# Moving a weight fold ahead of two gate blocks, splitting output weights on GpSimd, and keeping rotary tables in rotating small buffers

## The chip, the cores and the metric

The kernel runs on one core of a Trainium2 chip. The metric is the device time of one execution in microseconds, lower is better; the time before is the median of three runs. The engines are TensorE (PE, with its weight loads PEld), VectorE (DVE), ScalarE (ACT), GpSimd (POOL) and SyncE (SP), which issues most DMAs. A "q" behind an engine's name (SPq) is its instruction queue.

## The reference

One step of a two-layer hybrid backbone on 1024 latent and 256 context tokens of width 1024, ten tiles of 128 tokens. Layer 0 is attention with a gate, layer 1 Fourier mixing with a gate. Cut to layer 0, where the change lies:

```python
hl = modulate(rms_norm(xl, norm_g[0]), shl, scl)       # the same for the context tokens
qa, ka, va, ga, qb, kb, vb, gb = split_even(hl @ even_w_in[0])
qa, ka = apply_rope(rms_norm(qa, gq)), apply_rope(rms_norm(ka, gk))
qb, kb = apply_rope(qb), apply_rope(kb)                # rotary positions, latent tokens only
oa = dense_block_attention(qa, [ka, ka_ctx], [va, va_ctx])                 # mixer A, global
ob = window_attention_with_ctx(qb, kb, vb, kb_ctx, vb_ctx, sink)           # mixer B, +-128 tokens
xl = xl + gate * (concat([oa * silu(ga), ob * silu(gb)]) @ even_w_out[0])
...
u, gate = split(h @ odd_w_in)                          # layer 1
x = x + gate * ((real(fft2(u)) * silu(gate)) @ odd_w_out)
```

## The kernel before, in words

All matrix products are in single precision split in two parts: `split` makes a high part (a rounded copy) and a low part (source minus high part) of each operand, and `mm3` runs three matmuls for a product. The strings given to `split` name the engines: "a" is ACT, "d" DVE, "p" POOL, and a longer string is a cycle.

Layer 0 runs as a stream of attention units. A unit is (tile t, group g, head pair pr): groups 0 and 1 are mixer A's key and value heads, 2 and 3 mixer B's. `soft` makes the scores on PE, their running maxima on DVE and the exponentials on ACT; `weigh` transposes the probabilities on PE (`pt`), copies them out on ACT with the low part on DVE, multiplies with the values (`av`), and leaves the result in a small buffer `e` (the copy L1060 on ACT and the sum L1062 on DVE) until a DMA to `od` (L1068) has taken it. After a tile's last unit `totals` makes the reciprocal row sums, which also pass through an `e` buffer (L1030) on their way to `scd`.

Everything else of layer 0 is filler. `fl_`, a `Filler`, holds a queue of pieces with a cost each. After every unit, `pump` adds that unit's credit (4.4 for most units of mixer A, 2.9 for mixer B's) and issues pieces from the head of the queue as long as the credit covers their cost and their `ready` condition holds; a head that is not ready holds up all behind it. The order of the queue is:

- the projections in the order of `ORDER`: query blocks `qa`, `qb`, key and value block `kb`, and the gate blocks `g0` to `g3`, each of 256 columns. `loader` loads the next block's weights ahead of the work of the block before it, and `releaser` gives a block's buffers back;
- the last two blocks, `g2` and `g3`, are taken together by token group (two groups of 512 latent tokens, then the 256 context tokens); beside the second and third group `wout_next` loads and splits the output weights `w_out`, eight row blocks of two halves each, into the buffers that the normalised input leaves;
- the fold named in `FLATE`, `f3`: `fold_load` loads 256 rows of layer 1's first weight, and four times `fold_piece` multiplies a part of it with a DFT table (PE, `wa`, 8 matmuls), copies it out on ACT and writes it to `wd`. The other three folds are made at the start of the kernel;
- the output projections `proj_load` and `proj_step` (PE, `oz`), two tiles a pair. A `proj_load` fetches a tile's `od`, gate `gd`, row sums `scd` and residual `xp`, multiplies them (L1221, L1222) and splits the product. During attention these loads are issued from POOL and the multiplies run there; only the first two pairs may begin before the attention ends.

The code gives the order of each engine's work by priority; the final static order on each engine is that of a list scheduler, which may put a later piece ahead of one that isn't ready. Within an engine, instructions run in that order.

SBUF is cut by hand into zones of equal buffers: `u`, `w`, `q`, `pt`, `p`, `h` (nine of 512 columns, for raw weights and temporaries) and `e` (four of 256 columns). `take` gives the buffer that has been free the longest, and `drop` gives one back. The rotary tables, 8 tiles of 96 columns, are a tile of their own, loaded once at L590 and read by `rope_pair`.

Of the kernel before, what the change touches and what calls it, by code (L numbers as in the profile page):

```python
# [9 lines left out]
F32 = mybir.dt.float32  # L10
# [7 lines left out]
P = 128  # L18
# [1 line left out]
NT = 10  # L20
EPS = 1e-6
GROUPS = ((0, 4, 0), (4, 4, 0), (8, 2, 1))
ZONES = {"u": (26, 1032), "w": (8, 1032), "q": (2, 1024), "pt": (3, 1024), "p": (4, 1280), "h": (9, 512), "e": (4, 256)}
BIG = ("w", "q", "pt", "p", "u")
UV = ("u",)
FILL_A, FILL_B, LAG_A, LAG_B = 4.4, 2.9, 1, 2
E_PH, E_OH, E_OL, E_WO = "a", "a", "d", "a"
# [30 lines left out]
FC, XF = 1.3, False  # L58
# [2 lines left out]
PAIRS = ((0, 4), (2, 6), (3, 7), (1, 5), (8, 9))  # L61
FILL_C, NLATE = 2.9, 8
E_FQ, E_GD = "d", "d"
ORDER = "qa0 qa1 kb0 qb0 qb1 g0 g1 g2 g3"
FLATE = "f3"
AT_B = "s"
AT_F = (0, 1, 2)
AT_N, AT_Z = (0, 0, 3, 0, 3, 2, 2, 2, 2, 2, 3, 3, 3), ("p", "pt", "q")
# [71 lines left out]
def hybrid_step(ctx: ExitStack, tc: tile.TileContext, I, O):  # L140
    nc = tc.nc
    pe, act, dve, pool, sp = nc.tensor, nc.scalar, nc.vector, nc.gpsimd, nc.sync

    cp = ctx.enter_context(tc.tile_pool(name="const", bufs=1))
# [11 lines left out]
    def take(tag, shape, dt=F32):  # L156
        tags = (tag,) if isinstance(tag, str) else tag
        z = min((t for t in tags if spare[t]), key=lambda t: spare[t][0])
        i = spare[z].popleft()[1]
        size = 2 if dt == BF16 else 4  # L160
        for s in shape[1:]:
            size *= s
        assert size <= 4 * ZONES[z][1]
        made[0] += 1
        return Buf(z, i, up.tile(list(shape), dt, tag=f"{z}{i}", name=f"{z}{made[0]}", bufs=1))

    def drop(*bufs):
        for b in bufs:
            stamp[0] += 1
            spare[b.zone].append((stamp[0], b.idx))  # L170
# [50 lines left out]
    SU = cp.tile([P, NT, 16, 2], F32, name="SU")  # L221
    NM = cp.tile([P, NT, 8], F32, name="NM")
    pool.memset(SU, 0.0)
    rope = cp.tile([P, 8, 96], F32, name="rope")

    csw = take("e", (P, 8, 32))
    pool.memset(csw.a, 0.0)
# [53 lines left out]
    def split(dst_h, dst_l, src, hc="a", lc="p"):  # L281
        copy("hi" + hc, hc, dst_h, src)
        pick("lo" + lc, lc).tensor_sub(dst_l, src, dst_h)  # L283


    def load_w(src, width=256, tags="w", gap=None, lc=E_WL, each=None, later=None):
        out = []
        for kp in range(2):
            hi = take(tags, (P, 4, width), F32R)
            lo = take(tags, (P, 4, width), F32R)  # L290
            for j in range(2):
                r0 = (kp * 4 + j * 2) * P
                if width <= 256:
                    raw = take("h", (P, 2, width))
                else:
                    raw = take(("p", "pt", "q", "w"), (P, 2, width))
                if gap is None:
                    sp.dma_start(raw.a, src[r0 : r0 + 2 * P, :].rearrange("(j p) f -> p j f", p=P))
                else:
                    gap(raw, r0)  # L300
                if each is not None:
                    each(raw, kp * 4 + 2 * j)

                def fin(raw=raw, hi=hi[:, 2 * j : 2 * j + 2, :], lo=lo[:, 2 * j : 2 * j + 2, :]):
                    split(hi, lo, raw.a, XE["wh"], lc)
                    drop(raw)

                if later is None:
                    fin()
                else:  # L310
                    later.append(fin)
            out.append((hi, lo))
        return out

    def drop_w(w):
        for h, l in w:
            drop(h, l)
# [7 lines left out]
    def w0cols(c0):  # L325
        return I["w_in0"][:, c0 : c0 + 256]
# [209 lines left out]
    def fold_load(g, parts=1):  # L536
        if "f" not in fold:
            fold["f"] = take("h", (P, 2, 256))
            sp.dma_start(fold["f"].a, I["fch"])
        wu = [take("w", (P, 1024)) for j in range(2)]  # L540
        for h in range(parts):
            cols = slice(h * (1024 // parts), (h + 1) * (1024 // parts))
            for j in range(2):
                sp.dma_start(wu[j][:, cols], I["wuT"][(2 * g + j) * P : (2 * g + j + 1) * P, cols])
        return wu
# [38 lines left out]
    def small_loads(i):  # L584
        if i == 0:
            sp.dma_start(gT, I["gT"])
            sp.dma_start(bT, I["bT"])
            dve.tensor_scalar(bT1, bT[:, :, 8:16], 1.0, None, op0=ALU.add)
        elif i == 1:
            sp.dma_start(rope, I["rope"])  # L590
            sp.dma_start(gk, I["gk"].partition_broadcast(P))
            sp.dma_start(gq, I["gq"].partition_broadcast(P))
        else:
            sp.dma_start(sink, I["sink"].partition_broadcast(P))
            dve.tensor_scalar(nsink, sink, -1.0, None, op0=ALU.mult)
            mraw = take("h", (P, 384))
            sp.dma_start(mraw.a, I["mask"])
            dve.tensor_copy(maskf, mraw.a)
            drop(mraw)
# [98 lines left out]
        drop(ck)  # L698

    def rope_pair(y, n, t, t1, t2):  # L700
        cb = rope[:, t : t + 2, 0:32].unsqueeze(2).to_broadcast([P, 2, 2 * n, 32])
        pick("rope", XE["rope"]).tensor_mul(  # L702
            t1.rearrange("p t h (b c) -> p t (h b) c", b=2), y.rearrange("p t h (b c) -> p t (h b) c", b=2), cb
        )
        for b in range(2):
            o, i = 32 * b, 32 - 32 * b
            sb = rope[:, t : t + 2, 32 + o : 64 + o].unsqueeze(2).to_broadcast([P, 2, n, 32])
            pick("rope", XE["rope"]).tensor_mul(t2[:, :, :, o : o + 32], y[:, :, :, i : i + 32], sb)
        pick("radd", XE["radd"]).tensor_add(t1, t1, t2)

# [133 lines left out]
    fl_ = Filler()  # L844
    fl_.depth = 9
    ws = {}
# [250 lines left out]
                after(u0)  # L1097
            fl_.pump(budget(un))

    def out_weights(src, ks, tags, lc="pd"):  # L1100
        out = []
        for k in ks:
            hi, lo = take(tags, (P, D), F32R), take(tags, (P, D), F32R)
            for hf in range(2):
                raw = take("h", (P, 512))
                sl = slice(hf * 512, hf * 512 + 512)
                sp.dma_start(raw.a, src[k * P : (k + 1) * P, sl])
                split(hi[:, sl], lo[:, sl], raw.a, E_WO, lc)
                drop(raw)
            out.append((hi, lo))  # L1110
        return out

    order = [nm for nm in ORDER.split()]
# [3 lines left out]

    def loader(nm):
        def fn():
            ws[nm] = load_w(w0cols(base[nm[:-1]] + 256 * int(nm[-1])))  # L1120
            return 0
        return fn

    def releaser(nm):
        def fn():
            drop_w(ws[nm])
            return 0
        return fn

# [4 lines left out]

    def wout_next(n):
        for _ in range(n):
            fl_.add(0.0, lambda k=wk_left.popleft(): wout.extend(out_weights(I["w_out0"], (k,), UV)) or 0)

    for i, nm in enumerate(order[:-1]):
        j = int(nm[-1])  # L1140
        work = []
        if nm[0] == "q":
            m = "ab".index(nm[1])
            for t in range(0, NT, 2):
                if nm == "qa0" and t in (0, 2):
                    continue
                work.append((5.4, lambda t=t, nm=nm, m=m, j=j: q_pair(m, j, t, ws[nm], "g"), ("q", t, 2 * m + j)))
        elif nm == "kb0":
            for t in range(0, NT, 2):
                work.append((5.4, lambda t=t, nm=nm: kv_pair(1, t, ws[nm], "g"), ("kb", t)))  # L1150
        elif i < len(order) - 2:
            work += [gate_work(j, c, gi) for c in range(2) for gi in range(3)]
        if i > 0:
            fl_.add(0.0, loader(order[i + 1]))
        for w in work:
            fl_.add(*w)
        if i < len(order) - 2:
            fl_.add(0.0, releaser(nm))

    for gi in range(3):  # L1160
# [223 lines left out]
    def can_run(i, j):  # L1384
        r = pairs[i][j]

        def fn():
            if sum(len(spare[z]) for z in OB[0]) < NSP or i > EARLY:
                return False
            return all(finished.get(t, 99) + SPAN < clock[0] for t in USES[r])  # L1390
        return fn
# [5 lines left out]
    def load_to(n):  # L1397
        while loaded[0] <= min(n, 9):
            proj_load(*steps[loaded[0]])
            loaded[0] += 1  # L1400
        return 0


    def late_fold(nm):
        def fn():
            ws[nm] = fold_load(int(nm[1]))
            return 0
        return fn

    for n, nm in enumerate(FLATE.split()):  # L1410
        fl_.add(0.0, late_fold(nm))
        if n == 0:
            fl_.add(0.0, lambda: load_to(0), ready=can_run(0, 0))
        for k in range(4):
            fl_.add(FC, lambda k=k, nm=nm: fold_piece(int(nm[1]), k, ws[nm]))
    if not FLATE:
        fl_.add(0.0, lambda: load_to(0), ready=can_run(0, 0))
    for n, ij in enumerate(steps):
        if n == 8:
            fl_.add(0.0, lambda: wgs.append(load_w(I["w_g1"][:, 0:256], tags=BIG)) or 0)  # L1420
# [547 lines left out]
```

## Time and profile before

| what | value |
|---|---|
| median of 3 runs | 1189.43 us (1188.47 to 1189.45) |
| profiled execution: span | 1196.9 us |
| PE busy | 1159.1 us, 97% of the span |
| DVE busy | 834.5 us, 70% |
| ACT busy | 577.1 us, 48% |
| POOL busy | 286.0 us, 24% |
| mean granted TensorE clock | 0.990 |

The span runs from the first to the last instruction of one profiled execution; the profile gives no other time for that execution, and the median is of other runs, without a profile. A row of instructions gives the start and duration in us, the engine, the line, the operation, output and inputs by their names in the code (buffer numbers left out), the count, and in brackets the idle time of the engine before it and what ended it. A row of a stretch gives the busy time of each engine with its count of instructions, the granted clock of TensorE as a part of full speed, the share of the DMA engines' time and their GB/s. A row of a group gives the count, busy us and mean ns, and behind the bar's second part the idle time before them and what ended it.

### The profile page before, as it was taken

How to read it: one execution, taken by the hardware profiler on the slowest of the kernel's cores; microseconds unless marked ns; L12 is line 12 of the kernel's file. 1: busy time of each engine (PE TensorE's matmuls, PEld its weight loads, DVE VectorE, ACT ScalarE, POOL GpSimd, SP SyncE). 2: the span in 40 equal slices, each digit the busy share in tenths (PEclk: the TensorE clock that was granted, in tenths of full speed). 3: DMA queues.
4: the chain of work that ended last, by engine and by line, in shares of the span. 5: the costliest groups of instructions: out<-in, count | busy, mean ns of one | idle time of the engine just before them, and what ended most of it. 6: DMA issues, size and time to landing. Idle time of an engine off the chain costs nothing.

```text
span 1196.9 us, 22002 instructions
## 1 busy us (share of the span) xinstructions
PE 1159.1 (97%) x8103; PEld 1037.9 (87%) x8103; DVE 834.5 (70%) x2006; ACT 577.1 (48%) x1159; POOL 286.0 (24%) x272
## 2 busy tenths in 40 slices
PE   8999999999999999999999989998999999999997
PEld 6788899999999998899888878886878888998886
DVE  2489778787777776678888867777755964367543
ACT  4442555555656655556676654532364225333211
POOL 2255644512222230011010035200212226200001
PEclk9999999999999999999999989998998999999999
DMA  9978512323532232444354477774214435364321
GB/s 327 365 257 272 160 59 69 89 77 113 148 89 78 76 95 84 100 120 116 83 148 105 131 223 203 232 224 160 85 45 136 147 115 167 109 186 150 141 105 54
DMA packets 130096, 168.81 MB, mean 141 GB/s; under 512 B 26298, under 2 KB 86454, under 8 KB 129988
## 3 DMA queue, kind: packets, MB, share of 16 engines
q1 hardware_dynamic: 127476, 158.74, 43.5%
q0 software_dynamic: 2368, 8.39, 2.3%
q8 instruction: 64, 1.05, 0.4%
q14 instruction: 44, 0.36, 0.1%
q10 hardware_dynamic: 144, 0.26, 0.1%
HBM read 123.19 MB, written 44.16 MB: 140 GB/s over the span
## 4 chain that ended last, share of the span: by engine, by line
PE 80%; DMA 9%; DVE 5%; ACT 2%; issue 2%; SPq 1%; POOL 1%; POOLq 0%; DVEq 0%; ACTq 0%
PE of L265 9%; PE q L265 8%; PE av L1051 8%; PE pt L1045 8%; PE ga L265 7%; PE sL L928 5%; PE u L265 5%; PE oz L265 4%; PE g1E L265 4%; PE g1O L265 4%; PE kv L265 3%; PE sC L928 2%; PE wa L559 2%; PE g1c L265 2%; DMA h<-i_w_out 2%
## 5 line engine op out<-in xcount | busy, mean ns | idle before, releaser
L277 ACT ACTIVATE pt<-pt 128x512 fp32r<-128x512 f32 (+1 forms) x265 | 146.8, 575 | 107.0 <-PE pt L1045 60.2
L1048 DVE TENSOR_TENSOR pt<-pt,pt 128x512 fp32r<-128x512 f32 (+1 forms) x264 | 170.8, 658 | 37.7 <-ACT pt L277 36.8
L1051 PE MATMUL av<-pt,u 128*128 128x256 f32 x1008 | 167.1, 289 | 0.7 <-ACT pt L277 0.7
L1045 PE MATMUL pt<-identr,p 128*128 128x128 f32 x1008 | 157.4, 273 | 1.1 <-ACT p L969 0.8
L265 PE MATMUL q<-w,u 128*128 128x256 f32 x960 | 143.9, 287 | 0.0
L1051 PEld LDWEIGHTS av<-pt,u 128*128 128x128 f32 x1008 | 138.9, 190 | 4.6 <-ACT pt L277 0.9
L265 PEld LDWEIGHTS q<-w,u 128*128 128x128 f32 x960 | 126.8, 188 | 4.9 <-issue 0.8
L1045 PEld LDWEIGHTS pt<-identr,p 128*128 128x128 f32 x1008 | 119.7, 141 | 8.0 <-ACT p L969 1.0
L969 ACT ACTIVATE p<-p,nm 128x1280 f32<-128x1280 f32 (+1 forms) x80 | 95.5, 1194 | 63.1 <-DVE p L962 62.8
L265 PE MATMUL ga<-u,w 128*128 128x512 f32 (+1 forms) x576 | 124.1, 360 | 0.8 <-DVE byp L1024 0.5
L265 PEld LDWEIGHTS ga<-u,w 128*128 128x128 f32 x576 | 93.6, 188 | 15.2 <-ACT pt L277 1.2
L283 POOL TENSOR_TENSOR w<-h,w 128x512 fp32r<-128x512 f32 x38 | 51.1, 1360 | 143.4 <-DVE w L279 115.0
L928 PE MATMUL sL<-u,q 128*128 128x512 f32 x256 | 82.4, 411 | 2.0 <-DMA q<-qd 2.0
L969 ACT ACTIVATE p<-p,NM 128x640 f32<-128x640 f32 (+2 forms) x80 | 59.2, 740 | 39.5 <-DVE p L962 39.4
L928 PE MATMUL sC<-u,q 128*128 128x256 f32 x320 | 61.8, 294 | 1.6 <-DMA q<-qd 1.0
L962 DVE TENSOR_SCALAR_CACHE_REDUCE p<-sL 128x512 f32<-128x512 f32 x64 | 43.9, 685 | 23.2 <-PE sL L928 14.2
L962 DVE TENSOR_SCALAR_CACHE_REDUCE p<-sL,nm 128x512 f32<-128x512 f32 x64 | 47.7, 745 | 13.7 <-PE sL L928 12.9
L265 PE MATMUL oz<-u,w 128*128 128x512 f32 x192 | 57.3, 403 | 0.0
L283 POOL TENSOR_TENSOR u<-h,u 128x512 fp32r<-128x512 f32 x16 | 20.6, 1293 | 138.0 <-ACT u L277 133.9
L928 PEld LDWEIGHTS sC<-u,q 128*128 128x128 f32 x320 | 48.8, 189 | 5.5 <-issue 1.1
L265 PE MATMUL oz<-u,u 128*128 128x512 f32 x160 | 48.7, 405 | 4.0 <-ACT u L277 2.5
L702 POOL TENSOR_TENSOR h<-h,rope 128x512 f32<-128x512 f32 (+1 forms) x18 | 21.9, 1214 | 126.4 <-ACT h L785 80.5
(728 smaller groups left out, 2569.8 us busy)
## 6 DMA issues: line engine op xcount, KB each, us to landing
q<-qd SPq DMA_DIRECT2D x80, 256.0 KB
h<-i_w_in SPq DMA_DIRECT2D x40, 256.0 KB
p<-i_ada_w SPq DMA_DIRECT2D x18, 512.0 KB
h<-i_w_out SPq DMA_DIRECT2D x32, 256.0 KB
pt<-i_ada_w SPq DMA_DIRECT2D x15, 512.0 KB
qd<-pt SPq DMA_DIRECT2D x20, 256.0 KB
q<-i_ada_w SPq DMA_DIRECT2D x9, 512.0 KB
qd<-q SPq DMA_DIRECT2D x18, 256.0 KB
```

The costliest lines, as they stand in the source:

```text
L265: pe.matmul(out, a, b, start=i == 0, stop=i == n - 1)
L277: act.activation(out, in_, AF.Copy)
L283: pick("lo" + lc, lc).tensor_sub(dst_l, src, dst_h)
L559: pe.matmul(acc[:, i * 256 : i * 256 + 256], wu[j][:, c0 : c0 + P], f[:, j, :], start=j == 0, stop=j == 1)
L702: pick("rope", XE["rope"]).tensor_mul(t1.rearrange("p t h (b c) -> p t (h b) c", b=2), y.rearrange("p t h (b c) -> p t (h b) c", b=2), cb)
L928: pe.matmul(ps, q_at(q, s, hc), keys, start=s == 0, stop=s == 1)
L962: dve.tensor_scalar(p[i][:, end[i] : end[i] + n], ps, sign, last[i], op0=ALU.mult, op1=ALU.min, accum_out=c)
L969: act.activation(p[i][:, 0 : end[i]], p[i][:, 0 : end[i]], AF.Exp, bias=last[i], scale=-1.0, accum_out=SU[:, t, hd + i, 0:1],)
L1045: pe.transpose(tp[:, jj * 256 + i * P : jj * 256 + i * P + P], p[i][:, off : off + P], ident)
L1048: dve.tensor_sub(pt[:, 1, 0:n], tp[:, 0:n], pt[:, 0, 0:n])
L1051: pe.matmul(acc, vv, pt[:, s, jj * 256 : jj * 256 + 256], start=c + jj + s == 0, stop=c + jj == nt - 1 and s == 1,)
```

## The change

- `f3` moves from its own place behind the gates (`FLATE`) into `ORDER` between `g1` and `g2`. Its load now comes ahead of g1's gates, g2's load behind them and ahead of the fold's four pieces, and g3's load behind those. `load_to(0)`, the first projection's load, stands directly behind the gates and the output weights.
- `out_weights` gets a parameter for the engine of the high part; layer 0's output weights now have both parts on POOL ("p", "p") instead of the high part on ACT and the low part on POOL and DVE in turn. Layer 1's output weights keep their engines.
- The rotary tables are three `e` buffers (cosine, minus sine, sine; 32 columns for each of the 8 tiles) loaded by three DMAs. The zone `e` grows from four to seven buffers, and the three are dropped when the last query block `qb1` is released.

```diff
-ZONES = {... "e": (4, 256)}
+ZONES = {... "e": (7, 256)}
...
-ORDER = "qa0 qa1 kb0 qb0 qb1 g0 g1 g2 g3"
-FLATE = "f3"
+ORDER = "qa0 qa1 kb0 qb0 qb1 g0 g1 f3 g2 g3"
...
-    rope = cp.tile([P, 8, 96], F32, name="rope")
+    rope = [take("e", (P, 8, 32)) for _ in range(3)]
...
-            sp.dma_start(rope, I["rope"])
+            for i in range(3):
+                sp.dma_start(rope[i].a, I["rope"][:, i])
...
-        cb = rope[:, t : t + 2, 0:32].unsqueeze(2).to_broadcast([P, 2, 2 * n, 32])
+        cb = rope[0][:, t : t + 2, :].unsqueeze(2).to_broadcast([P, 2, 2 * n, 32])
...
-            sb = rope[:, t : t + 2, 32 + o : 64 + o].unsqueeze(2).to_broadcast([P, 2, n, 32])
+            sb = rope[1 + b][:, t : t + 2, :].unsqueeze(2).to_broadcast([P, 2, n, 32])
...
-    def out_weights(src, ks, tags, lc="pd"):
+    def out_weights(src, ks, tags, lc="pd", hc=E_WO):
...
-                split(hi[:, sl], lo[:, sl], raw.a, E_WO, lc)
+                split(hi[:, sl], lo[:, sl], raw.a, hc, lc)
...
     def loader(nm):
         def fn():
+            if nm[0] == "f":
+                ws[nm] = fold_load(int(nm[1]))
+                return 0
...
     def releaser(nm):
         def fn():
             drop_w(ws[nm])
+            if nm == "qb1":
+                drop(*rope)
...
-            fl_.add(0.0, lambda k=wk_left.popleft(): wout.extend(out_weights(I["w_out0"], (k,), UV)) or 0)
+            fl_.add(0.0, lambda k=wk_left.popleft(): wout.extend(out_weights(I["w_out0"], (k,), UV, "p", "p")) or 0)
...
+        elif nm[0] == "f":
+            work += [(FC, lambda k=k, nm=nm, j=j: fold_piece(j, k, ws[nm])) for k in range(4)]
...
-        if i < len(order) - 2:
+        if i < len(order) - 2 and nm[0] != "f":
             fl_.add(0.0, releaser(nm))
...
-    for n, nm in enumerate(FLATE.split()):
-        fl_.add(0.0, late_fold(nm))
-        if n == 0:
-            fl_.add(0.0, lambda: load_to(0), ready=can_run(0, 0))
-        for k in range(4):
-            fl_.add(FC, lambda k=k, nm=nm: fold_piece(int(nm[1]), k, ws[nm]))
-    if not FLATE:
-        fl_.add(0.0, lambda: load_to(0), ready=can_run(0, 0))
+    fl_.add(0.0, lambda: load_to(0), ready=can_run(0, 0))
```

The host's table is stored as (partition, table, tile, 32) instead of (partition, tile, 96).

More of the change, by code (lines that the diff above doesn't have):

```diff
@@ L22 @@
 GROUPS = ((0, 4, 0), (4, 4, 0), (8, 2, 1))
-ZONES = {"u": (26, 1032), "w": (8, 1032), "q": (2, 1024), "pt": (3, 1024), "p": (4, 1280), "h": (9, 512), "e": (4, 256)}
+ZONES = {"u": (26, 1032), "w": (8, 1032), "q": (2, 1024), "pt": (3, 1024), "p": (4, 1280), "h": (9, 512), "e": (7, 256)}
 BIG = ("w", "q", "pt", "p", "u")
@@ L1401, in load_to @@
         return 0
[L1404 to L1408, printed above, removed]
-    for n, nm in enumerate(FLATE.split()):
-        fl_.add(0.0, late_fold(nm))
-        if n == 0:
-            fl_.add(0.0, lambda: load_to(0), ready=can_run(0, 0))
-        for k in range(4):
-            fl_.add(FC, lambda k=k, nm=nm: fold_piece(int(nm[1]), k, ws[nm]))
-    if not FLATE:
-        fl_.add(0.0, lambda: load_to(0), ready=can_run(0, 0))
+    fl_.add(0.0, lambda: load_to(0), ready=can_run(0, 0))
     for n, ij in enumerate(steps):
@@ L1918 @@
     an = np.concatenate([ar, ac], axis=1)
-    rope = np.concatenate([np.cos(an), -np.sin(an), np.sin(an)], axis=1).reshape(8, 128, 96).transpose(1, 0, 2)
+    rope = np.concatenate([np.cos(an), -np.sin(an), np.sin(an)], axis=1).reshape(8, 128, 3, 32).transpose(1, 2, 0, 3)
     i = np.arange(128)
```

## Prediction

> **What bounds the kernel now.** I read the shares of busy time first, then the busy time of each engine in stretches, then the chain of waits, and last the single instructions of the stretches that lose time.
>
> ```profile
> span 1196.9 us, 22002 instructions
> PE 1159.1 (97%) x8103; PEld 1037.9 (87%) x8103; DVE 834.5 (70%) x2006; ACT 577.1 (48%) x1159; POOL 286.0 (24%) x272
> ```
>
> TensorE (PE) is busy 97% of the span, and the change removes none of its matmuls. So only two things can move the time: PE idle time, and matmuls that run at a lower granted clock. The whole span has 1196.9 - 1159.1 = 37.8 us of idle. The profiled execution's span is 7.5 us (0.6%) above the median of the three runs, 1189.43 us; my terms are differences read in that span and taken off the median. A difference under 0.2% (2.4 us) is about what a measurement of this kernel can't tell from none.
>
> The edits act from about 560 us (the gates of mixer B's phase) to 840 us (the first output projections). Busy time by stretch there:
>
> ```profile
> core 0: us, PE busy (x) PEld busy (x) DVE busy (x) ACT busy (x) POOL busy (x), PEclk, DMA share, GB/s
> 600.00:690.00 90.00, 87.55 (x592) 79.31 (x591) 76.68 (x236) 61.05 (x142) 9.84 (x8) 1.00 0.48 126
> 690.00:720.00 30.00, 24.54 (x146) 22.27 (x145) 18.09 (x56) 17.25 (x43) 11.76 (x15) 0.89 0.81 228
> 720.00:800.00 80.00, 77.17 (x422) 65.48 (x421) 62.41 (x141) 38.09 (x86) 20.96 (x17) 1.00 0.73 221
> 800.00:840.00 40.00, 35.57 (x150) 28.27 (x150) 27.46 (x35) 11.23 (x16) 2.89 (x3) 0.91 0.51 167
> ```
>
> PE idle is 2.45, 5.46, 2.83 and 4.43 us, and in the second and fourth the granted clock is 0.89 and 0.91. All that can be won lies here: about 15 us of idle and some 6 us of clock.
>
> The largest hole is at 693.8 us. PE, ACT and SyncE's queue (SPq) in order of time:
>
> ```profile
> 690.53 0.38 SPq L1107 DMA_DIRECT2D h<-i_w_out  x1
> 696.75 0.63 ACT L277 ACTIVATE u<-h 128x512 fp32r<-128x512 f32 x1 [6.60 <-DMA h<-i_w_out]
> 697.55 0.59 ACT L277 ACTIVATE pt<-pt 128x512 fp32r<-128x512 f32 x1
> 698.27 3.75 PE L559 MATMUL wa<-h,w 128*128 128x256 f32 x8 [4.51 <-ACT pt L277]
> 701.82 1.06 PE L1045 MATMUL pt<-identr,p 128*128 128x128 f32 x4
> 705.28 0.60 PE L1045 MATMUL pt<-identr,p 128*128 128x128 f32 x4
> 713.56 1.89 PE L559 MATMUL wa<-h,w 128*128 128x256 f32 x8
> ```
>
> ACT's next instruction was the high-part copy of an output weight whose DMA had only just been issued. ACT waited 6.60 us, the attention's copies (`pt<-pt`) stood behind it, and PE stood 4.51 us behind those. The eight fold matmuls after it took 3.75 us, the last eight 1.89 us, and the first four transposes 1.06 against 0.60: a further 1.86 + 0.46 = 2.3 us. The Trainium skill (TensorE: Matmul & The Clock Gate, Why this matters for your kernels) says to avoid idle gaps above about 3 us between matmul bursts, since the clock then falls back to half; 3.75 against 1.89 agrees.
>
> **Output weights on GpSimd.** In 600 to 700 us, ACT, VectorE (DVE) and GpSimd (POOL) spend on the 16 half-row pieces:
>
> ```profile
> L277 ACT ACTIVATE u<-h 128x512 fp32r<-128x512 f32 x16 | 9.9, 629 | 19.7 <-DMA h<-i_w_out 16.9 <-PE ga L265 1.5 <-PE sC L928 1.3
> L283 DVE TENSOR_TENSOR u<-h,u 128x512 fp32r<-128x512 f32 x8 | 5.5, 683 | 1.9 <-ACT u L277 1.9
> L283 POOL TENSOR_TENSOR u<-h,u 128x512 fp32r<-128x512 f32 x8 | 10.3, 1293 | 111.9 <-ACT u L277 107.7 <-PE sB L1000 4.2
> L350 POOL MEMSET u<- 128x1024 f32 x2 | 1.8, 956 | 11.9 <-PE oz L265 11.9
> ```
>
> ACT loses 9.9 us of work and 16.9 us of waiting for these DMAs, DVE 5.5 us. POOL gets 16 copies and 8 more subtractions. No row shows a POOL copy: it lies between half of a memset of 1024 columns (0.48 us) and the two-input subtraction (1.29). I take 0.9, between write-only and two reads. POOL then does 16 x 0.9 + 16 x 1.293 = 35 us (28 to 41) instead of 10.3, on an engine busy 9.84 of 90 us; behind its waits stand only its own later work, the projection's loads and multiplies. The hole of 4.51 us, its 2.3 us of clock, and 1 of the 2.45 us of small idles should go: of 600 to 720 us' loss, 2.45 + 5.46 + 2.3 = 10.2 us, the remainder that I keep is 1.4 us.
>
> **The fold ahead of the last gates.** Nothing is removed: 32 matmuls (four pieces of 1.89 us, 7.6 us), four ACT copies, four `wd` writes, three loads (`fch`, two `wuT`). All move from behind the last gates to behind g1's, near 570 us, on PE, ACT and SPq. The load of g2 now comes behind g1's gates, and g3's behind the fold:
>
> ```profile
> 565.92 5.04 POOL L283 TENSOR_TENSOR w<-h,w 128x512 fp32r<-128x512 f32 x4 [25.17 <-ACT w L277]
> ```
>
> This is such a split today, g3's, begun when g1's last gate freed the weight buffers. It ends some 6 us after they are free (5.04 of subtractions behind the first copy). The four fold pieces alone, 7.6 us on PE, cover it; uncovered it would cost 6 us. I take 0.
>
> What matters is the place that the fold leaves. Between the last gate and the first projection PE has, besides attention, only the fold:
>
> ```profile
> 690.28 0.60 PE L265 MATMUL ga<-u,w 128*128 128x256 f32 x3
> 718.10 5.73 PE L265 MATMUL oz<-u,w 128*128 128x512 f32 x24
> 689.24 0.78 POOL L1215 DMA_DIRECT2D u<-od  x1 [4.26 <-PE ga L265]
> 697.47 1.26 POOL L283 TENSOR_TENSOR u<-h,u 128x512 fp32r<-128x512 f32 x1 [6.91 <-ACT u L277]
> 699.74 0.55 POOL L1218 DMA_DIRECT2D u<-gd  x1
> 705.41 2.37 POOL L1221 TENSOR_TENSOR u<-u,u 128x1024 f32<-128x1024 f32 x1 [4.58 <-DMA u<-gd]
> 700.00:720.00 20.00, 19.04 (x111) 17.34 (x111) 15.34 (x48) 13.90 (x35) 8.67 (x10) 0.89 0.84 221
> ```
>
> The projection's buffers come free with the last gate (POOL waits for `ga`), and from there load, two multiplies and split take 27 us. Without ACT's stall POOL doesn't wait its 6.91 us; I take a gap of 23 us (16, if the fold's DMAs gone from a stretch with 0.84 DMA share help too; 27, if nothing does). Without the fold the gap is attention alone. In 700 to 720 us PE's 19.04 us hold about 7.7 of fold and 1.9 of projection, so 9.4 of attention, for which DVE needed 15.34 less a projection split of 1.2, 14.1 us. DVE therefore lets PE be busy 67%, and 23 us cost 23 x 0.33 = 7.6 us (5.3 to 8.9). The idle comes in pieces under 1 us, so I take no clock loss. This gives back most of the 10.2 us: the cover was worth nearly as much as the stall.
>
> **Three more small buffers from the end of rotation.** The total stays: 3 x 256 columns against 8 x 96. From the end of rotation on, 7 `e` places rotate instead of 4. The waits for `od` writes to leave such a buffer, and what PE did near them:
>
> ```profile
> 729.53 0.42 DVE L1062 TENSOR_TENSOR e<-av,e 64x256 f32<-64x256 f32 x1 [3.17 <-DMA od<-e]
> 732.13 2.89 DVE L283 TENSOR_TENSOR u<-w,u 128x1024 fp32r<-128x1024 f32 x1
> 734.52 2.73 POOL L1222 TENSOR_TENSOR w<-w,w 128x1024 f32<-128x1024 f32 x1
> 758.58 1.23 DVE L283 TENSOR_TENSOR u<-w,u 128x1024 fp32r<-128x1024 f32 x1 [2.31 <-ACT u L277]
> 736.84 3.71 PE L265 MATMUL oz<-u,u 128*128 128x512 f32 x15 [1.59 <-DVE h L1243]
> 809.40 1.23 DVE L1221 TENSOR_TENSOR u<-u,u 128x1024 f32<-128x1024 f32 x1 [5.57 <-DMA u<-gd]
> 810.83 0.27 ACT L1030 ACTIVATE e<-tt 16x128 f32<-16x128 f32 x1 [9.54 <-DMA od<-e]
> 815.78 0.55 PE L1274 MATMUL eoE<-identr,p 128*128 128x128 f32 x3 [1.96 <-DVE p L1370]
> 818.78 1.22 PE L265 MATMUL oz<-u,u 128*128 128x512 f32 x2 [2.45 <-ACT u L277]
> ```
>
> The 3.17 us on DVE stand ahead of the 1.59 us on PE; with them gone I take -1.6 (0 to -1.6). The 9.54 us on ACT delay the last row sums by as much, but PE's 1.96 and 2.45 us hang on DVE, which at the same time waited 5.57 us for a gate load that SPq issued late. 800 to 840 us loses 4.4 of idle and 0.09 x 40 = 3.6 of clock, 8 us; the change can win between 0 and 8, and since the nearest wait is not the buffer's, I take a quarter, -2.
>
> One rule speaks against the -1.6. DVE's split at 732.13 took 2.89 us where its like took 1.23, while POOL multiplied beside it. The Trainium skill (GPSIMD Engine Reference, Specifications) says that GpSimd shares its SBUF interfaces with VectorE and contends with VectorE instructions that have two SBUF inputs. The two rows agree with it. If this alone made the 1.59 us, my sum is 1.6 us higher, 1186.7.
>
> **Rotary tables.** One transfer becomes three, on SPq:
>
> ```profile
> 54.15 0.66 SPq L590 DMA_DIRECT2D rope<-i_rope  x1
> 60.00:80.00 20.00, 19.57 (x177) 18.26 (x177) 14.93 (x29) 9.10 (x16) 11.32 (x9) 1.00 0.86 301
> ```
>
> Two more issues hold SPq's later loads by up to 1.3 us, where PE is busy 19.57 of 20: between 0 and +1.3, I take +0.5. The strides of the rotation change, not its shapes: 0.
>
> **Sum.** -10.2 + 1.4 (ACT's stall) + 7.6 (gap without fold) - 1.6 - 2 (small buffers) + 0.5 (loads) = -4.3 us: 1185 us, 0.4% less.
>
> **Rivals.** No change: the gap stays at 27 us (8.9), and neither the 1.6 nor the 2 come, as the late link is SPq. Then -10.2 + 1.4 + 8.9 + 0.5 = +0.6, about 1190. For it: the 5.57 us row. Against it: POOL's 6.91 us are ACT's.
>
> Better: the later start of the projections leaves fewer attention units beside them, and the last row sums come 9.54 us sooner, so that the whole 8 us after 800 us go, and the gap shrinks to 16 us (5.3). Then -10.2 + 1.4 + 5.3 - 1.6 - 8 + 0.5 = -12.6, 1177.
>
> Slower: POOL becomes the late link. The last eight pieces come beside the four context gates, 668.7 to 690.9 us, and POOL needs 8 x 2.2 = 17.5 us (21 at the upper price) of those 22. If it is behind when the last gate ends, the projection's loads and multiplies queue behind it, and the raw pieces stay in `h`, so that SPq stands at the next load with the q loads behind it:
>
> ```profile
> SPq L1107 <- POOL u L283: 4.5, 3, 2.1
> 668.69 3.04 PE L265 MATMUL ga<-u,w 128*128 128x256 f32 x24 [0.31 <-ACT pt L277]
> 716.64 0.71 PE L928 MATMUL sC<-u,q 128*128 128x256 f32 x4 [0.96 <-DMA q<-qd]
> ```
>
> SPq waits 4.5 us so today with 8 of 16 pieces on POOL, each 1.29; with 16 at 2.2 it is about 15 us. If PE sees half of the added 11 us (5.5), the gap grows by 8 us (2.6), and one idle piece reaches 4 us (2.3 of clock): -4.3 + 10.4 = +6.1, 1195. It decides once POOL's lag at the last gate costs PE about 7 us in these ways. Against it: POOL has 90 us for 35 us of work.
>
> **Chances.** Forecast and better 0.55 (0.12 of it better), no change 0.22, slower 0.23. That POOL's contention keeps the 1.6 us I give 0.1 of the 0.55. The likeliest's own range is 1180 to 1187. The range over all, 1177 to 1195, leaves out about 2 in 10.
>
> **What would show it.** No ACT wait for `i_w_out` in the attention phase, and no PE hole of 4 us there; the fold near 570 to 590 us; from last gate to first projection some 23 us, with PE about two thirds busy and DVE full; no wait of ACT or DVE for `od<-e`. It is wrong if that gap holds PE holes over 3 us, if POOL's splits end many us after their loads land, if SPq waits for POOL more than 10 us, or if the time moves outside 560 to 840 us, since instructions of other stages could be ordered anew.

## The result, and the profile after

The changed kernel takes 1206.74 us (median of 4, 1201.91 to 1207.82) against 1189.44 us for the kernel before (4 executions): ratio 1.0125, 95% interval 1.0099 to 1.0151 (the two medians by themselves give 1.0145). It is slower by 1.25%, where 0.4% faster was forecast and 1195 us was the upper end of the range. The profiled execution of the changed kernel is the fastest of the four (1201.91 us, span 1200.1).

The executions of the kernel before lie 8 to 12 us apart within one study (1186.11 to 1200.09 us over all of them), but for one of 3948.68 us and, of the run "fold earlier" below, the profiled one with a span of 4282.7 us, whose times are not read.

The span of the first profile of before, 1196.9 us, is 7.4 us above that of a second one, 1189.5 us (its time 1191.29), so I compare with the second. In it, TensorE's holes from the last gates to the first projection (the timeline of PE; the bracket is the idle time before the row and what ended it):

```profile
694.51 0.60 PE L265 MATMUL ga<-u,w 128*128 128x256 f32 x3
697.84 1.89 PE L559 MATMUL wa<-h,w 128*128 128x256 f32 x8
702.33 1.89 PE L559 MATMUL wa<-h,w 128*128 128x256 f32 x8
706.61 1.89 PE L559 MATMUL wa<-h,w 128*128 128x256 f32 x8
710.18 0.48 PE L928 MATMUL sC<-u,q 128*128 128x256 f32 x2 [1.67 <-DMA q<-qd]
712.07 1.89 PE L559 MATMUL wa<-h,w 128*128 128x256 f32 x8
715.96 4.35 PE L265 MATMUL oz<-u,w 128*128 128x512 f32 x18
```

The 4.51 us hole ahead of the fold, on which the forecast's largest term stood, is not there: all four fold pieces take 1.89 us. The same stretch of the changed kernel:

```profile
573.95 1.89 PE L558 MATMUL wa<-h,w 128*128 128x256 f32 x8
583.93 1.89 PE L558 MATMUL wa<-h,w 128*128 128x256 f32 x8
702.03 3.05 PE L264 MATMUL ga<-u,w 128*128 128x256 f32 x24
722.55 0.77 PE L928 MATMUL sC<-u,q 128*128 128x256 f32 x2 [7.70 <-DMA q<-qd]
739.85 0.63 PE L264 MATMUL oz<-u,w 128*128 128x512 f32 x2
742.05 5.36 PE L264 MATMUL oz<-u,w 128*128 128x512 f32 x22 [0.76 <-DVE w L282]
```

The fold ran at 574 to 586 us, as forecast. The last gate ends at 705.08 and the first `oz` starts at 739.85. In this gap TensorE waits 7.70 us for a `q` load; in a second profile of the changed kernel (e5 below) it is 8.58 us. Busy time of the engines from the first `av` to the last gate, in the gap, and from the first to the last `oz`, first the changed kernel, then the second profile of before (stretch, its length, busy time of PE, PEld, DVE, ACT, POOL, granted clock, DMA share, GB/s):

```profile
143.36:705.08 561.72, 557.24 (x4107) 524.46 (x4106) 427.94 (x1152) 335.08 (x661) 142.47 (x138) 1.00 0.37 101
705.08:739.85 34.77, 22.96 (x149) 20.71 (x148) 23.99 (x75) 18.74 (x46) 17.63 (x18) 0.85 0.83 213
739.85:869.27 129.42, 125.98 (x603) 103.33 (x601) 98.13 (x158) 48.65 (x95) 24.19 (x20) 1.00 0.56 180
```

```profile
144.22:695.11 550.89, 545.99 (x4026) 512.69 (x4025) 425.29 (x1140) 331.19 (x652) 122.82 (x113) 1.00 0.36 99
695.11:715.96 20.85, 18.87 (x129) 17.49 (x129) 16.79 (x49) 16.01 (x37) 9.26 (x10) 1.00 0.95 276
715.96:860.31 144.35, 139.87 (x699) 116.90 (x697) 110.12 (x207) 61.33 (x124) 32.51 (x29) 0.98 0.61 188
```

The difference of the two spans, 10.6 us, is made up so, from the first `av` (143.36; before 144.22), the end of the last gate, the first and the last `oz` (869.27; before 860.31) and the end: start -0.9, up to the last gate +10.8, gap +13.9, projections -14.9, remainder +1.6. These stretches do not hold the same work, though. The 7.6 us of fold matmuls now stand ahead of the last gate, and so do 16 more of the attention's 1008 `av` matmuls (908 instead of 892); attention done in the gap is missing beside the projections later. Since both kernels have the same matmuls, the loss shows in TensorE's idle time (the length less PE's busy time) and in its clock. The idle time is 4.5 us up to the last gate (before 4.9), 11.8 in the gap (2.0) and 3.4 beside the projections (4.5). Over the whole span it is 43.2 us against 34.0, which is 9.2 of the 10.6 us. So the loss lies in the gap: 9.8 us more of idle, and a clock of 0.85 over 34.8 us, by estimate 5.2 us (0.15 x 34.8), of which the projections give back about 4 (1.0 of idle, and 0.02 x 144 = 2.9 of clock).

Up to the last gate the idle time has not grown, but one hole in it is new (the first row, timeline of PE; the second, chain of waits):

```profile
555.30 4.88 PE L264 MATMUL ga<-u,w 128*128 128x512 f32 x20 [1.91 <-ACT e L1060]
548.95 4.29 DMA h<-i_w_in
```

g2's load, which the change puts behind g1's gates, is on the path there; I had costed it at nothing.

On GpSimd the change does what it says (groups of instructions, 590 to 710 us):

```profile
L282 POOL TENSOR_TENSOR u<-h,u 128x512 fp32r<-128x512 f32 x16 | 20.5, 1296 | 0.2
L278 POOL CAST u<-h 128x512 fp32r<-128x512 f32 x16 | 9.8, 615 | 86.0 <-DMA h<-i_w_out 44.7 <-PE ga L264 41.4
```

A copy takes 0.61 us, less than the 0.9 that I took. GpSimd waits for the data, and no wait of ScalarE for `i_w_out` is left. SyncE's queue, however, waits for GpSimd once (waits of SP, 640 to 712 us):

```profile
SPq L1107 <- POOL u L282: 4.5, 1, 4.5
```

It stands 4.5 us at an output weight's load, until 700.81 us, and from there issues what had gathered behind it without a pause, up to the first of the `q` loads that come late, at 706.40. The other three profiles with both the fold and GpSimd's part have this wait too (4.8, 4.7 and 5.2 us in e5, e6 and e11 below); with GpSimd's part alone it is at most 0.4 us (e3, e17), with the fold alone 3.8 us in two parts (e2, e16). That it makes `q` late was not tried by a run.

### The profile page after: what moved, and what is told of

Its sections match the earlier page's. It is cut to its first block, busy times and chain, and to the rows that moved or that the text cites. A ratio compares the mean times of both kernels' runs of the same rounds, so it can differ in the third digit from the quotient of the medians.

```text
span 1200.1 us, 21995 instructions
## 1 busy us (share of the span) xinstructions
PE 1156.9 (96%) x8103; PEld 1036.3 (86%) x8103; DVE 832.9 (69%) x1994; ACT 572.0 (48%) x1147; POOL 305.8 (25%) x296
## 4 chain that ended last, share of the span: by engine, by line
PE 80%; DMA 10%; DVE 6%; ACT 1%; issue 1%; SPq 1%; POOL 0%; POOLq 0%; DVEq 0%; ACTq 0%
PE of L264 9%; PE ga L264 9%; PE av L1051 9%; PE q L264 8%; PE pt L1045 8%; PE oz L264 7%; PE u L264 5%; PE sL L928 5%; PE g1E L264 3%; PE kv L264 3%; PE sC L928 3%; PE g1O L264 3%; DMA q<-qd 2%; DMA h<-i_w_in 2%; PE g1c L264 1%; PE sB L1000 1%
## 5 line engine op out<-in xcount | busy, mean ns | idle before, releaser
L962 DVE TENSOR_SCALAR_CACHE_REDUCE p<-sL 128x512 f32<-128x512 f32 x64 | 43.9, 686 | 24.0 <-PE sL L928 14.9
L702 POOL TENSOR_TENSOR h<-h,e 128x512 f32<-128x512 f32 (+1 forms) x18 | 21.9, 1217 | 125.6 <-ACT h L785 79.7
L962 DVE TENSOR_SCALAR_CACHE_REDUCE p<-sC,nsink 128x256 f32<-128x256 f32 x80 | 37.5, 474 | 20.6 <-PE sC L928 16.5
L264 PE MATMUL oz<-u,w 128*128 128x512 f32 x192 | 50.9, 395 | 0.8 <-DVE w L282 0.8
L264 PE MATMUL of<-u,u 128*128 128x512 f32 x150 | 50.3, 394 | 0.0
```

Source lines behind the costliest of these rows:

```text
L264: pe.matmul(out, a, b, start=i == 0, stop=i == n - 1)
L702: pick("rope", XE["rope"]).tensor_mul(t1.rearrange("p t h (b c) -> p t (h b) c", b=2), y.rearrange("p t h (b c) -> p t (h b) c", b=2), cb)
L962: dve.tensor_scalar(p[i][:, end[i] : end[i] + n], ps, sign, last[i], op0=ALU.mult, op1=ALU.min, accum_out=c)
```

## The experiments

Ratios are to the kernel before, run on the same chip, with the 95% interval; 0.2% is 2.4 us. Three theories went in: the fold was the cover of the gap (T1), GpSimd's new work is the late link (T2), the table buffers cost (T3).

**Each part alone, and the kernel before against itself.**

```
e1: no edit
e2: ORDER = "... g0 g1 f3 g2 g3", FLATE = "", loader/releaser/work for f3 as in the diff
e3: out_weights(I["w_out0"], (k,), UV, "p", "p")
e4: ZONES "e": (7, 256); rope = three takes of "e"; drop(*rope) after qb1
```

> The kernel before, unchanged, for a second profile. The first profile had a span of 1196.9 us, 7.5 us above the median of the unprofiled runs, and a PE hole of 4.51 us behind an ACT wait of 6.60 us for an output weight. If that hole belongs to every execution, this profile shows it again, with a span near 1196. If it was that one execution's, the span comes near 1188, the ACT wait is under 3 us, and most of the gain that was forecast was never there to be had.

> Only the fold is moved ahead of the last gates. Theory 1 (the fold was the cover of the way from the last gate to the first projection, and q loads now fall into the projections' loads with nothing else for PE): slower by 8 to 18 us, with a PE wait for a q load of several us in that gap. Theory 2 (POOL as the late link) and theory 3 (rotary tables and small buffers): within 3 us of before.

> Only layer 0's output weights go to POOL for both parts; the fold stays last. Theory 1: same or faster by up to 5 us, because ACT's waits for the weights' DMAs go and the fold still covers the gap. Theory 2: slower by 5 us or more, with POOL's splits ending long after the weights land and the projection's loads behind them. Theory 3: no change.

> Only the rotary tables in three small buffers that are given back after rotation. Theories 1 and 2: within 3 us of before, a little faster if the waits of DVE and ACT for a small buffer cost anything. Theory 3: slower by 5 us or more, with the loss at the start (three transfers instead of one) or in the order of the attention phase.

Measured: e1 0.9988 (0.9967 to 1.0009); e2, the fold, 1.0074 (1.0049 to 1.0099); e3, GpSimd, 0.9984 (0.9964 to 1.0004); e4, the tables, 1.0049 (1.0029 to 1.0069). T2 falls as far as GpSimd's part alone goes. The fold costs some 9 us, the tables some 6, GpSimd nothing.

**Two at a time, and all again.**

```
e5: the changed kernel   e6: fold + GpSimd   e7: fold + tables   e8: GpSimd + tables
```

> The changed kernel, unchanged, for a second profile and times beside its parts. Its first profile is of its fastest execution, 1201.91 us, where the others took 1206 to 1208. Theory 1: the PE wait for a q load in the gap is there again, longer when the time is longer.

> The change without the rotary tables. Theory 1: about the time of the fold moved alone. Theory 2: the time of the whole change. Theory 3: near before.

> The change without POOL's splitting. Theory 1: about the time of the fold moved alone. Theory 2: near before. Theory 3: the time of the whole change.

> The change without the fold's move. Theory 1: no slower than before, as the fold is back as cover of the gap, and faster by up to 6 us if ACT's waits and the small buffers cost anything. Theories 2 and 3: slower by 5 us or more.

Measured: e5 1.0096 (1.0063 to 1.0129), e6 1.0104 (1.0067 to 1.0141), e7 1.0113 (1.0068 to 1.0157), e8 1.0063 (1.0040 to 1.0085). Fold and tables add up: 0.74 + 0.49 = 1.23 against 1.13 for the two together, and 0.96 and 1.25 for the whole change in two studies. The intervals are too wide to say how much each still costs beside the others.

**The tables kept to the end.** The same three places, transfers and reads, but nothing is given back, so that four `e` places rotate as before.

```
-            if nm == "qb1":
-                drop(*rope)
```

> Three rotary tables in small-buffer places, loaded by three transfers, rotation reading them there; but they are never given back, so that four places rotate to the end, as before. Theory (what costs is the longer ring after rotation: with seven places the order of instructions from 690 us on becomes another one, with a PE hole of some 5 us behind DVE near 815 us): with four places the order stays, no PE hole over 3 us behind ssp in 800 to 840 us, ACT's wait of 9 us for od<-e is back, ratio to before 0.998 to 1.002. Rival (the three transfers at the start, or the rotation's strides): 1.004 to 1.006 as with the tables alone, first oz near 718 us or later already before the projections, av first 1 to 2 us later than before's 144.

Measured: 1.0012 (0.9989 to 1.0035). The cost of the tables is the giving back, not the transfers or the strides. What it did, in the timelines of PE and DVE of the tables-only kernel, then PE and ACT of this one:

```profile
815.53 1.22 PE L1052 MATMUL av<-pt,u 128*128 128x256 f32 x4 [5.30 <-DVE ssp L1354]
813.92 1.22 DVE L1224 TENSOR_TENSOR q<-q,u 128x1024 f32<-128x1024 f32 x1 [2.16 <-DMA u<-scd]
815.07 0.41 DVE L1063 TENSOR_TENSOR e<-av,e 64x256 f32<-64x256 f32 x1
815.40 0.13 DVE L1354 COPY ssp<-ss 128x1 f32<-128x1 f32 x1
```

```profile
811.87 0.55 PE L1275 MATMUL eoE<-identr,p 128*128 128x128 f32 x3 [1.96 <-DVE p L1371]
814.87 1.22 PE L265 MATMUL oz<-u,u 128*128 128x512 f32 x2 [2.45 <-ACT u L277]
806.94 0.27 ACT L1031 ACTIVATE e<-tt 16x128 f32<-16x128 f32 x1 [9.95 <-DMA od<-e]
```

With seven places the instructions from about 595 us on stand in another order: 195 of VectorE's 2006 are at another place of its list than in before. With the tables kept, the lists of TensorE, VectorE and ScalarE are those of before. ScalarE's wait for `od<-e`, 9.95 us with four places, is gone in that form; but the evacuation of `av` (`e<-av,e`) now stands on VectorE behind a multiply that waits for `scd`, and TensorE's last `av` behind that, 5.30 us (the profile names the small copy `ssp` that follows the evacuation). With four places TensorE has the 1.96 and 2.45 us of before. In the 40 us from 800 us TensorE idles 6.9 us at a clock of 0.87, with the tables kept 4.6 us at 0.96: 2.3 us of idle and by estimate 3.6 of clock (0.09 x 40), about the 5.1 us between the two spans (1196.6 and 1191.5). The wait that the change takes away was off the path, and the order that came with it was not. That the order, and not the number of places as such, makes the 5.30 us is read from these rows; it was not tried by itself.

**The fold at both places.** The fold ahead of g2 and g3, and f3 done once more at the old place (its table's buffer is given back after the fifth fold as well).

```
-FLATE = ""          # of the fold-only kernel
+FLATE = "f3"
```

> The fold alone moved ahead of g2 and g3, and the same fold done once more at its old place (32 matmuls, 7.6 us of PE, its loads, copies and writes, all twice). Theory (the fold at its old place filled time in which PE stands otherwise): the repeat costs far less than its 7.6 us beyond the fold-only kernel (1.0074), ratio 1.005 to 1.010, the share of idle between last gate and first oz falls. Rival (the cost of the move lies where the fold now stands, and the old place was no cover): 7.6 us more than fold only, ratio 1.013 to 1.016.

Measured: 1.0171 (1.0137 to 1.0204), some 10 us above fold only (1.0074 and, below, 1.0092): against the cover theory as I had put it, and a little above the rival's range. The trace shows both halves (timeline of PE):

```profile
714.57 2.35 PE L559 MATMUL wa<-h,w 128*128 128x256 f32 x8
726.12 0.47 PE L928 MATMUL sC<-u,q 128*128 128x256 f32 x2 [1.28 <-DMA q<-qd]
727.69 1.89 PE L559 MATMUL wa<-h,w 128*128 128x256 f32 x8
753.47 6.27 PE L265 MATMUL oz<-u,u 128*128 128x512 f32 x20 [4.50 <-DVE h L1248]
813.95 0.81 PE L265 MATMUL oz<-u,p 128*128 128x512 f32 x2 [2.35 <-DVE h L1248]
```

In the gap the repeat is covered: 23.7 us from the end of the last gate (708.29) to the first `oz` (731.99), in the two fold-only profiles 23.8 and 21.9. It comes back behind the projections' multiply on VectorE (`h`), with holes of 4.50 and 2.35 us. Why is open.

**The second projection's gate and sums not loaded**, in the changed kernel (e11) and in the kernel before (e12).

```
+            if r != 4:   # else: tensor_mul(ol, ol, ol) twice, no gd, no scd
                 ld.dma_start(gl.a, gate[r])
```

> The changed kernel, with the second projection (row block 4) left without its gate and sums: their loads (gd, two of scd, 1 MB of some 2 MB) are not made, its two multiplies are kept, on the attention output alone. The second projection's result is therefore another. Theory (q's transfers of 256 KB take 12 us and more because the loads of both first projections are issued at the same time): the PE wait for q<-qd of 7 to 8.6 us between last gate and first oz falls under 3 us, ratio 1.004 to 1.008. Rival (the gap is set by the first projection's own chain of load, multiply and split, and q is late for its own reason, the issue on SPq): a wait for q of over 5 us stays, ratio 1.009 to 1.013.

> The kernel before with the same part left out (gate and sums of row block 4 not loaded): the control of the run before this one. Theory (the loads collide with q only where no fold delays and covers): 0.997 to 1.000. Rival (the loads cost the same in both kernels): 0.993 to 0.996, and the changed kernel gains no more than this one.

Measured: e11 1.0068 (1.0045 to 1.0092), e12 1.0047 (1.0029 to 1.0066). The ratio of e11 fits the theory, its trace does not:

```profile
722.20 0.76 PE L928 MATMUL sC<-u,q 128*128 128x256 f32 x2 [7.40 <-DMA q<-qd]
```

The hole stays with 1 MB less to load. These loads are not what makes `q` late. The Trainium skill (DMA: Bandwidth & Descriptors, Issuing engines are not separate DMA queues) says that transfers issued by different engines run on the same 16 DMA engines and interleave; that this is what delays `q` no run here shows. And the control became slower by 5.6 us for less work, by neither theory.

How long a `q` load takes is seen in the chain of waits, in the second profile of before, then in the changed kernel:

```profile
698.00 1.74 PE wa L559 x8
699.98 10.06 DMA q<-qd
```

```profile
706.40 12.31 DMA q<-qd
718.73 3.84 DMA q<-qd
```

In the kernel before, too, the load took 10.06 us. Two fold pieces (702.33 and 706.61) and attention lay beside it, and TensorE waited 1.67 us.

**Only the matmuls of the fold, taken away at either place; the fold at a third place; fold only once more.**

```
e13: ORDER = "qa0 qa1 kb0 f3 qb0 qb1 g0 g1 g2 g3"
e14, e15: fold_piece of f3 without its pe.matmul; copy("wo", "a", wo, <from f>) 
e16: as e2
```

> The fold moved further ahead: between kb0 and qb0, in the stretch before 520 us where PE has no idle, and g2's and g3's loads behind the gates as in before. Theory A (the old place was nearly free, any earlier place pays the fold's 7.6 us): last gate about 8 us later, gap as in the fold-only kernel, ratio to before 1.005 to 1.010. Theory B (the new place is what costs: the load of g2 behind g1's gates and the holes after it): 0.998 to 1.002, and no PE idle of 1.9 us in 520 to 560 us.

> The kernel before with the 32 matmuls of fold f3 left out, at its old place behind the last gates; its loads, copies and writes stay (the copies read the fold's table instead). Theory A (PE time of the fold at the old place is nearly free): ratio 0.997 to 1.001. Theory B (PE time counts there as anywhere): 7.6 us less, ratio 0.993 to 0.995.

> The fold-only kernel with the same 32 matmuls left out, at the new place ahead of g2 and g3; loads, copies and writes stay. Theory A: the full 7.6 us come back, 0.999 to 1.002, close to the kernel before. Theory B (what costs at the new place is g2's load and the order, not PE's time): most of the 9 us stay, with g2's load less covered, 1.004 to 1.009.

> The fold's move alone once more, on the chip of the three runs before it: ratio 1.005 to 1.010 (1.0074 the first time); a profiled execution nearer its median, last gate some 10 to 13 us later after the first av than in before, and from there to the last oz about as long as in before, by either theory.

Measured: e13 1.0158 (1.0128 to 1.0188), e14 1.0046 (1.0029 to 1.0063), e15 1.0021 (1.0002 to 1.0039), e16 1.0092 (1.0062 to 1.0123).

At the old place, leaving out 7.6 us of matmuls wins nothing, it loses 0.46%; at the new place it gives back 1.0092 - 1.0021 = 0.7%, 8.5 us. The time comes back where the matmuls stood: from the first `av` to the last gate e16 takes 562.5 us, e15 552.2. That is theory A, the matmuls were free behind the last gates and cost their full time ahead of g2, with one miss: e14 should have stayed within 0.1% and is above it. The trace of e14 shows the cover gone (timeline of PE; then the gap's busy times of e14 and of e16):

```profile
712.79 1.19 PE L928 MATMUL sC<-u,q 128*128 128x256 f32 x4 [4.97 <-DMA q<-qd]
```

```profile
695.05:719.83 24.78, 17.79 (x111) 14.77 (x110) 17.38 (x56) 15.47 (x38) 9.17 (x9) 0.93 0.85 255
```

```profile
706.30:728.22 21.92, 16.26 (x111) 14.70 (x109) 18.00 (x59) 14.51 (x38) 10.75 (x10) 0.92 0.92 252
```

The wait for `q` that the fold had covered to 1.67 us is 4.97, and the gap is 24.8 us long with 7.6 us less to do. Leaving out matmuls has also changed the planned order (119 of VectorE's 2006 instructions stand elsewhere than in before, from 699 us on), so how much of the 4.97 us is the missing cover alone is not shown. In e16 the gap without the fold is 21.92 us, with it in before 20.85: 7.6 us of work left, and the time stayed. The 10.4 us by which e16's span exceeds that of before (1199.9 to 1189.5) lie up to the last gate, +11.6; gap +1.1, projections -2.2. Counted by TensorE's idle time it is +1.8 up to the last gate, +3.7 in the gap and +0.6 beside the projections; the rest is clock (0.989 against 0.993).

e13 misses both: 19 us slower, where A gave at most 12 and B none. A place further from the gap is no better, and g2's load alone is not the cost; what makes it worse than e2 is open, since the times of its trace can't be compared.

**GpSimd once more, and its copies alone.**

```
e17: as e3          e18: out_weights(I["w_out0"], (k,), UV, "pd", "p")   # subtractions alternate as before
```

> Output weights' copies and subtractions on GpSimd, nothing else changed; once more, in five rounds. Theory (ACT's waits for i_w_out stood off the path in most executions, so their going brings little): ratio 0.997 to 1.000. Rival (the forecast's 8.8 us were there): 0.992 to 0.994.

> Only the high-part copies of the output weights go from ScalarE to GpSimd; the subtractions stay alternating between GpSimd and VectorE. ACT's waits for i_w_out go here as well, GpSimd gets 16 copies of 0.61 us (10 us) and no more subtractions. Theory (what there is to win is ACT's wait): same as with both, 0.997 to 1.000. Rival (VectorE's 5.5 us of subtractions are what counts): 0.999 to 1.002, above the run before it.

Measured: e17 1.0001 (0.9985 to 1.0017), e18 1.0106 (1.0083 to 1.0128). GpSimd's part by itself is no version that beats the kernel before; none of the runs is. e18 misses both theories: with eight subtractions left on VectorE the kernel is 12 us slower than e17. Its holes, after e17's:

```profile
704.39 0.48 PE L928 MATMUL sC<-u,q 128*128 128x256 f32 x2 [3.27 <-DMA q<-qd]
708.36 0.71 PE L928 MATMUL sC<-u,q 128*128 128x256 f32 x4 [1.22 <-DMA q<-qd]
```

```profile
690.59 0.47 PE L928 MATMUL sC<-u,q 128*128 128x256 f32 x2 [4.31 <-DMA q<-qd]
711.71 0.77 PE L928 MATMUL sC<-u,q 128*128 128x256 f32 x2 [4.53 <-DMA od<-e]
```

TensorE waits 8.8 us in two holes for DMAs, and the clock from 680 to 720 us is 0.91; in e17 it waits 4.5 us in two shorter ones, at 1.00. Where each `q` load stands in the queue differs from kernel to kernel.

## Why the prediction was wrong

The sum had three parts: GpSimd -10.2 + 1.4 = -8.8, the fold +7.6, the tables -1.6 - 2 + 0.5 = -3.1. Measured alone: GpSimd -1.9 and +0.1 us (e3, e17), the fold +8.8 and +11.0 (e2, e16), the tables +5.8 (e4). Two parts failed; the fold's was right in size alone, but not beside GpSimd's.

**GpSimd, -10.2.** The mechanism was there: ScalarE's waits for `i_w_out` are gone, 13.9 us of them in the second profile of before, 16.9 in the first. The failed step is "the hole of 4.51 us, its 2.3 us of clock ... should go": they belonged to one execution of the kernel before, the one that was 7.5 us above the median. The second profile has no such hole, nor has that of the tables-kept kernel, whose TensorE, VectorE and ScalarE run in the order of before. I had written that the execution was slow, and then took a difference read in it off the median. What made it slow was, in part, such holes: TensorE idles 37.8 us in the first profile and 34.0 in the second, 3.8 of the 7.4 us between their spans. (The terms named as going, 4.51 + 2.3 + 1, also make 7.8 us, not the 8.8 of the sum.) What GpSimd's part wins ahead of the last gate is lost behind it. In e17 (the same three stretches as above):

```profile
142.50:688.14 545.64, 544.20 (x4033) 513.20 (x4032) 419.48 (x1133) 324.16 (x638) 143.26 (x138) 1.00 0.37 101
688.14:712.40 24.26, 19.55 (x132) 17.98 (x132) 19.80 (x56) 15.65 (x38) 10.94 (x12) 1.00 0.91 245
712.40:859.20 146.80, 140.02 (x690) 115.99 (x689) 104.92 (x199) 60.94 (x122) 31.37 (x27) 0.98 0.59 181
```

TensorE's idle time falls by 3.5 us up to the last gate (1.4 against 4.9) and rises by 2.7 in the gap and 2.3 beside the projections. Of the rival "POOL becomes the late link", which put 1195, one sign is there: SyncE's queue waits 4.5 us for GpSimd at an output weight's load, where it forecast about 15. By itself GpSimd's part costs nothing, so this rival is not what made the change slow alone; what the wait does beside the fold is open.

**The fold, +7.6.** For the fold alone the term held: the gap of 23 us is 21.9 in e16, and 5.66 us of idle with 0.08 x 21.9 = 1.8 us of clock make 7.4. In the whole change the same gap loses 11.8 us of idle and by estimate 5.2 of clock, 17.0 in place of the 7.6. Three points failed. "The idle comes in pieces under 1 us, so I take no clock loss": it comes with the `q` loads, in holes of 1.8 and 3.3 us in e16 and 7.70 in the changed kernel, where the clock is 0.85 over the gap. The 7.70 us are beyond the idle gaps of about 3 us that the Trainium skill warns of (TensorE: Matmul & The Clock Gate, Why this matters for your kernels); the trace agrees. Shorter holes cost clock here as well: in e3 it is 0.50 from 705 to 710 us, after no hole above 2.13 us. The gap of the changed kernel is 34.8 us, above my bound of 27. I had taken GpSimd's part to shorten the gap (its wait of 6.91 us gone); beside the fold it goes with more idle there, 10.9 to 12.7 us with both (e6, e5) against 5.7 and 6.9 without GpSimd's part (e16, e7), though the ratios of these runs do not differ beyond their intervals. And g2's load, costed at 0, leaves holes of 1.7 to 2.05 us.

**The tables, -3.1.** Wrong in sign. I priced the wait that goes, 9.54 us on ScalarE, and gave a quarter of it to the path, though the row of VectorE's 5.57 us said which wait ended last. I did not price that a longer ring lets the planner order the later instructions anew; the prediction named that only as what could make it wrong.

**The sequence of proofs.** The giving back is shown as the tables' cost (e4, e9). That the fold's matmuls cost their time at the new place is shown by e15 and e16; that they were free at the old place is supported by the gap of e16 and by e14, which won nothing, but whose order changed as well. Against it stands the repeat (e10), whose 10 us came back later in the projections. What decides that, and why e12, e13, e14 and e18 are slower by half a per cent to 1.6%, is open. A rival that none of the runs sets aside is the planner: in each of them it orders the instructions anew (VectorE's list differs from before's from 731 us on in e12, 699 in e14, 612 in e18). But it does so in e17 too, from 611 us on, without a loss, so a new order is a possible cause and not a shown one.

## What to carry to other kernels

A hole that one profile shows is worth what it costs in the usual execution: where the profiled execution is a per cent above the median, take a second profile of the same kernel before pricing its largest stall. Matmuls that stand where their engine waits for loads anyway can be nearly free there; moved into a full stretch they cost their time, here 8.5 us for 7.6, and the wait that they covered appears. Where a change moves work, compare the bounding engine's idle time and clock by stretch, not the stretches' lengths. Giving buffers back to a ring let the planner reorder what takes from it here, so look at what the wait would be replaced by, not only at the wait.

## What was not expected of the hardware

A GpSimd copy of 128x512 into fp32r took 0.61 us, less than half of its two-input subtraction (1.30 us). A 256 KB load of `q` took 10 to 12 us while the projections' loads ran, and cutting 1 MB of these left the hole at 7.40 us. Leaving work out made this kernel slower twice, each time in a new planned order: 1.0047 without 1 MB of loads (e12), 1.0046 without 32 matmuls (e14).
